# A hybrid transformer layer on one core: the residual gates multiply results in place of the weights w_out and w_down

## The chip, the cores and the metric

The kernel runs on one core of a Trainium2 chip. The metric is the time of one execution on the device, in microseconds (us); the median of several executions is compared.

The core's engines run side by side, each through a fixed list of instructions of its own: TensorE (PE in the profile; PEld is its weight load) does matmuls into PSUM, VectorE (DVE), ScalarE (ACT) and GpSimd (POOL) work element by element, and SyncE (SP) issues the DMA transfers, in the order of its list: a transfer whose turn has come but whose buffer is not free holds up all that stand behind it.

## The reference, cut to what matters

One layer on 2048 latent positions of 1024 channels, in float32:

```python
ada = jnp.einsum('bd,lde->lbe', jax.nn.silu(c), w_ada) + b_ada[:, None, :]
sh1, sc1, g1, sh2, sc2, g2 = (m[:, None, :] for m in jnp.split(ada[l], 6, axis=-1))
...
h = modulate(rmsnorm(x, norm_mix[l]), sh1, sc1)
o, _, _ = token_mixers(h @ w_in[l], ...)              # gated recurrence, and a spatial gating unit
x = x + g1 * (o @ w_out[l])                           # w_out: 1024 x 1024
h2 = modulate(rmsnorm(x, norm_ffn[l]), sh2, sc2)
x = x + g2 * conv_ffn(h2, w_up[l], conv_w[l], conv_b[l], w_down[l], rows)   # w_down: 2816 x 1024
...
return rmsnorm(x, norm_final)
```

g1 and g2 are vectors over the 1024 output channels. So g1 * (o @ w_out) is the same as o @ (w_out * g1), each column of the weight being multiplied by its gate, and likewise for g2 and w_down.

## The kernel before, in words

Each float32 product is made of three matmuls on split operands: `split(hi, lo, raw)` lets ACT round a tile to `hi` (a CAST) and another engine, POOL unless one is named, subtract: `lo = raw - hi`; `mm3` then adds up hi x hi, hi x lo and lo x hi. A right operand is 512 columns wide.

The work is done in stages.

- Stage 1 (0 to about 1036 us): input projection, the recurrence's heads and the gating unit's heads. The weights of w_in are split in 128x1024 tiles (`whi`, `wlo`); the results, transposed, go to DRAM (`oT`). Behind it runs a background queue, `bg_q`, a list of generators that are advanced as the matmuls are written out: a number that a generator yields is the amount of PE time to let pass before its next step. It holds `ada_block` (the gates; g1 and g2 end up in DRAM as the two rows of `g_d`), `w_out_ops`, `conv_taps` and `w_down_ops`.
- `w_out_ops` loads w_out in sixteen 128x512 pieces, each with a broadcast of its part of g1, multiplies (DVE), splits (ACT, DVE) and stores both halves to DRAM (`wo_d`). `w_down_ops` loads w_down in 22 pieces of 128x1024, multiplies by g2 (DVE) and stores them to `wd_d`.
- The handover: `open_wo` opens the pool for the output projection. The split w_out, eight tiles `wo` of 1 MB (128 rows of w_out each, both halves), is loaded from `wo_d`, three of them early, into buffers that the heads have left (`wo_early`). The first tile of `o` is loaded through a raw buffer and split by ACT and DVE.
- The output projection (1036 to 1230): 16 tiles of 128 positions; in each, two halves of the columns (n) and in each half eight k, with three matmuls each: 48 matmuls `dn<-wo,o`. DVE adds the result to x (`xn`, shown as `cv<-dn,raw`), SP stores it, ACT squares it (L1255). After every second tile `second_norm` follows: POOL makes `rs`, DVE scales both tiles of `xn` (L1176), PE transposes them (`up<-ident,cv`, or `dn<-ident,cv` for the last pair), and the results, split, are stored as `yd`, from where the far operands `yl` and `yh` are loaded.
- The up-projection and the convolution (1230 to 2108) are not touched.
- The down-projection (2108 to 2533): by a scheme with seven products of half sums, in seven phases (q = 0 to 6) of NJ = 11 steps with 8 result tiles each. `load` fetches the operands of a step three steps ahead, `prepare` forms the sums and differences of two weight blocks (`sT`, in a ring `wr()` of five, or a resident one) and activations (`mr`, `sS`) and splits them (`mhl`, `th`, `tl`). After the last step of a phase `evict` adds the 8 results to `odd` or `even` rows, `sums_behind` and `odd_rows` do the rest in the steps that follow.

The order of the instructions on each engine is fixed when the program is built, by a scheduler that follows the order in which they are written and a model of the time that passes.

Of the kernel before, what the change touches and what calls it, by code (L numbers as in the profile page):

```python
# [18 lines left out]
P = 128  # L19
# [53 lines left out]
def tile_trunk(ctx, tc, x, c, cx, c_ctx, w_ada, b_ada, norm_mix, norm_ffn, w_in, hg_norm, sgu_g, sgu_b,  # L73
# [31 lines left out]
    xl_d = dr.tile([P, NK, TH], F32, name="xl_d")  # L105
    wo_d = dr.tile([P, NK, 2, D], F32, name="wo_d")
    wd_d = [dr.tile([P, 2, D], F32, name=f"wd{j}") for j in range(NF // 2)]
    xn_d = [dr.tile([P, D], F32, name=f"xn{i}") for i in range(2 * NCH)]
# [69 lines left out]
    with es1:  # L178
# [634 lines left out]

        def wo_load(t):
            ld(t.bitcast(F32), wo_d[:, len(wo)])
            wo.append(t)

        def wo_early(tag):
            wo_load(pk.tile([P, 2, D], F32R, tag=tag, name="wo", bufs=2 if tag == "K" else 1, align_bytes=AL))

# [67 lines left out]

        def w_out_ops():

            todo = [(k, slice(n * 512, n * 512 + 512)) for k in range(NK) for n in range(2)]
            raws = []

            def load(i):
                if i < len(todo):
                    k, cl = todo[i]
                    raw = raw_tile()
                    ld(raw[:, :512], w_out[k * P:(k + 1) * P, cl])
                    ld(raw[:, 512:], g_d[0:1, cl].broadcast_to([P, 512]))
                    raws.append(raw)  # L900
            load(0)
            yield 5.0
            for i, (k, cl) in enumerate(todo):
                load(i + 1)
                raw = raws.pop(0)
                w, g = raw[:, :512], raw[:, 512:]
                hi = pm.tile([P, 512], F32, tag="acc", name="wo_hi")
                pin(V.tensor_mul(w, w, g))
                split(hi.bitcast(F32R), g.bitcast(F32R), w, V)
                st(wo_d[:, k, 0, cl], hi)  # L910
                st(wo_d[:, k, 1, cl], g)
                yield 7.0

        def w_down_ops():

            for n in range(2):
                cl = slice(n * 512, n * 512 + 512)
                g = pm.tile([P, 512], F32, tag="acc", name="g2")
                ld(g, g_d[1:2, cl].broadcast_to([P, 512]))
                for j in range(NF // 2):  # L920
                    raw = raw_tile().rearrange("p (a c) -> p a c", a=2)
                    ld(raw, w_down[2 * j * P:2 * (j + 1) * P, cl].rearrange("(a p) c -> p a c", p=P))
                    yield 9.0
                    pin(V.tensor_mul(raw, raw, view(g, 0, [[0, 2], [1, 512]])))
                    st(wd_d[j][:, :, cl], raw)
                    yield 2.5

        def silu(dst, scale):
# [6 lines left out]
        def head(hh, h):  # L935
# [16 lines left out]
            def pre_g():  # L952
                if prev[0] >= 0:
                    need(hg_q, (prev[0], prev[1], "keys"))
                else:
                    need(bg_q, "x1")
                    for e in range(8):
                        bg_q.add(ada_block(e))
                    bg_q.add(w_out_ops())
                    bg_q.add(conv_taps())  # L960
                    bg_q.add(w_down_ops())
                t["F"] = pk.tile([P, 2, TH], F32, tag="F", name="F", align_bytes=AL)
                t["K"] = pk.tile([P, 2, TH], F32, tag="K", name="K", bufs=2, align_bytes=AL)
# [77 lines left out]
        def open_wo():  # L1041
            hg_q.drain()
            bg_q.drain()
            esh.close()
            pw = esw.enter_context(tc.tile_pool(name="pw", bufs=1, side="right", reuse_waits="tile"))
            first_o.append(lambda: pw.tile([P, 2, NK, P], F32R, tag="o", name="o", align_bytes=AL))
            early = len(wo)

            def load():
                raw = raw_tile().rearrange("p (k c) -> p k c", c=P)  # L1050
                ld(raw, oT_d[0][:, :, 0:P])
# [119 lines left out]
    with tc.tile_pool(name="po", bufs=1, reuse_waits="tile") as po:  # L1171
# [49 lines left out]
        def fetch_x(t):  # L1221
            xt = raw_tile2(2 if t == nt_ - 1 else 1 + 2 * (t % 2))
            ld(xt.rearrange("p a b -> p (a b)"), x[t * P:(t + 1) * P, :])
            return xt.rearrange("p a b -> p (a b)")

        raw_o = {1: fetch_o(1)}
        xts = {0: fetch_x(0)}
        ops = {0: first_o[1]}
        xs = []
        for t, (hh, g) in enumerate(tiles):  # L1230
# [21 lines left out]
            xn = v_tile()[:, :D]  # L1252
            V.tensor_add(xn, pd.rearrange("p a b -> p (a b)"), xts.pop(t))
            st(xn_d[t], xn)
# [167 lines left out]
    def b_src(c, n, j):  # L1422
        return wd_d[j][:, c, n * 512:(n + 1) * 512]

# [82 lines left out]
    even = [pd_.tile([P, 2, 512], F32, name=f"even{i}") for i in range(NCH)]  # L1507
    nf = pd_.tile([P, D], F32, name="nf")
    nw = [0]
    ra, rb = {}, {}  # L1510
# [52 lines left out]
    def prepare(n):  # L1563

        if n >= 7 * NJ:
            return
        q, j = divmod(n, NJ)
        (a, b), (a2_, b2) = ra.pop(n), rb.pop(n, (None, None))
        if q == 4:
            V.tensor_sub(a, a, a2_)  # L1570
            V.tensor_sub(b, b, b2)
        cast(n, a, b, slot_s(n), slot_t(n))
        S_, T_ = sS[:, j, :], sTj(j)
        if q == 1:
            V.tensor_add(S_, a2_, S_)
            V.tensor_sub(T_, b2, T_)
        elif q == 2:
            V.tensor_sub(S_, S_, a2_)
            V.tensor_sub(T_, b2, T_)
        elif q == 3:  # L1580
            V.tensor_sub(S_, a2_, S_)
        elif q == 5:
            V.tensor_sub(T_, T_, b2)
# [45 lines left out]
    def sums_behind(q, i):  # L1629
        o, e = odd[i], even[i]  # L1630
        if q == 1:
            side.append(lambda: V.tensor_add(e[:, 0, :], e[:, 0, :], o[:, 0, :]))
        elif q == 3:
            def f():
                V.tensor_add(e[:, 1, :], e[:, 1, :], o[:, 0, :])
                V.tensor_add(e[:, 1, :], e[:, 1, :], o[:, 1, :])
            side.append(f)
        elif q == 4:
            def f():
# [14 lines left out]
    def evict(q, i, pd):  # L1654
        o, e = odd[i], even[i]
        if q in (0, 2):
            S.copy(o[:, q // 2, :], pd)
        elif q in (1, 5):
            V.tensor_add(e[:, q // 5, :], pd, e[:, q // 5, :])
        elif q in (3, 4):  # L1660
            V.tensor_add(o[:, 0, :], pd, o[:, 0, :])
# [65 lines left out]
```

## Time and profile before

| | us |
|---|---|
| median of 3 executions | 2530.53 |
| lowest, highest | 2528.71, 2533.55 |
| span of the profiled execution | 2532.6 |
| PE busy | 2450.9 (97%) |
| DVE busy | 1802.1 (71%) |
| POOL busy | 1063.7 (42%) |
| ACT busy | 960.3 (38%) |

The DMA queues move 400.13 MB. A time of the profiled execution by itself is not listed; its span, from the first to the last instruction, lies 0.95 below the highest of the three times and 2.1 above their median. Busy time is read as a share of the span: with PE at 97%, what is left for a change that keeps the matmuls is PE's idle time and the stretches in which the clock that PE was granted is below full.

### The profile page before, as it was taken

What the parts mean: (1) busy time and instruction counts of PE and PEld (TensorE: products, weight loads), DVE (VectorE), ACT (ScalarE), POOL (GpSimd) and SP (SyncE); (2) the same over time, 40 slices, a digit from 0 to 9 for tenths busy, and PEclk for the clock granted to TensorE, in tenths of its full rate; (3) what the DMA queues carried; (4) which work ended last, traced back from release to release, by engine and by line L of the source; (5) the groups of instructions that cost most, each with busy time, mean ns of one, the idle gap of its engine ahead of it and who ended that gap; (6) DMA issues with size and microseconds to landing.
All of it is one profiled execution on the core that took longest, in us unless ns stands there. A gap on an engine that the chain in (4) does not pass through costs nothing.

```text
span 2532.6 us, 32806 instructions
## 1 busy us (share of the span) xinstructions
PE 2450.9 (97%) x11859; PEld 2022.7 (80%) x11859; DVE 1802.1 (71%) x2375; ACT 960.3 (38%) x1598; POOL 1063.7 (42%) x871
## 2 busy tenths in 40 slices
PE   7999999999999999999999999999999999999998
PEld 4788888878888888788778888878878887888786
DVE  5866775735756757465699778749999993676775
ACT  2554334434334333255443333324333342332252
POOL 1444232322333433100587887877878870000002
PEclk8999999999999999999999999999999999999999
DMA  8365334583353422667932222472222248844744
GB/s 291 100 190 175 118 116 157 182 293 112 112 163 112 153 96 88 225 220 248 309 101 89 89 84 89 140 267 84 81 91 92 88 144 331 275 144 139 227 155 149
DMA packets 305838, 400.13 MB, mean 158 GB/s; under 512 B 33025, under 2 KB 216057, under 8 KB 301965
## 3 DMA queue, kind: packets, MB, share of 16 engines
q1 hardware_dynamic: 302420, 397.30, 47.4%
q8 instruction: 94, 1.54, 0.2%
q10 hardware_dynamic: 3257, 0.75, 0.1%
q14 instruction: 67, 0.55, 0.1%
HBM read 288.85 MB, written 109.13 MB: 157 GB/s over the span
## 4 chain that ended last, share of the span: by engine, by line
PE 39%; DVE 6%; DMA 2%; POOL 2%; issue 1%; ACT 0%; SPq 0%; POOLq 0%; ACTq 0%; DVEq 0%
PE up L65 24%; PE dn L65 15%; DVE dn L1315 3%; DVE edges L1320 1%; DMA raw<-in_w_up_dram 1%; DMA sT<-wd 1%; POOL Al L121 1%; DVE gp L1391 0%; DMA yl<-yd 0%; POOL cv L1402 0%; DVE odd L1595 0%; DMA mr<-m 0%; POOL raw L1142 0%; ACT dn L1612 0%; DVE cv L1399 0%
## 5 line engine op out<-in xcount | busy, mean ns | idle before, releaser
L1315 DVE SCALAR_TENSOR_TENSOR dn<-gp,taps,dn 128x1024 f32<-128x1024 f32 x352 | 448.2, 1280 | 20.5 <-ACT dn L1312 17.3
L121 POOL TENSOR_TENSOR Al<-raw,Ah 128x512 fp32r<-128x512 f32 x264 | 344.8, 1313 | 97.4 <-ACT Ah L120 88.9
L65 PE MATMUL pj<-xh,whi 128*128 128x512 f32 x896 | 366.4, 409 | 2.1 <-ACT whi L120 1.6
L65 PE MATMUL pj<-xl,whi 128*128 128x512 f32 x896 | 353.4, 395 | 3.7 <-DMA xl<-xl_d 1.8
L65 PE MATMUL pj<-xh,wlo 128*128 128x512 f32 x896 | 353.2, 394 | 2.7 <-POOL wlo L121 1.7
L65 PE MATMUL dn<-th,mhl 128*128 128x512 f32 x1120 | 349.9, 393 | 4.4 <-ACT mhl L120 2.4
L65 PE MATMUL up<-xah,Ah 128*128 128x512 f32 x704 | 277.5, 394 | 1.7 <-ACT Ah L120 1.3
L65 PE MATMUL up<-xah,Al 128*128 128x512 f32 x704 | 276.8, 393 | 2.0 <-POOL Al L121 2.0
L65 PE MATMUL up<-yl,Ah 128*128 128x512 f32 x704 | 274.6, 390 | 2.1 <-DMA yl<-yd 2.1
L120 ACT CAST Ah<-raw 128x512 fp32r<-128x512 f32 x264 | 160.4, 618 | 295.9 <-PE up L65 243.5
L65 PEld LDWEIGHTS dn<-th,mhl 128*128 128x128 f32 x1120 | 211.7, 189 | 50.7 <-ACT mhl L120 2.8
L121 POOL TENSOR_TENSOR wlo<-raw,whi 128x1024 fp32r<-128x1024 f32 x56 | 144.1, 2574 | 243.2 <-ACT whi L120 198.2
L113 POOL TENSOR_SCALAR rs<-ss 128x2 f32<-128x2 f32 (+1 forms) x16 | 7.7, 479 | 534.4 <-ACT jk L1587 366.0
L65 PE MATMUL dn<-tl,mhl 128*128 128x512 f32 x560 | 220.6, 394 | 0.0
L65 PE MATMUL up<-yh,Ah 128*128 128x512 f32 x528 | 208.1, 394 | 0.0
L65 PE MATMUL up<-yh,Al 128*128 128x512 f32 x528 | 206.9, 392 | 0.0
L65 PE MATMUL up<-xal,Ah 128*128 128x512 f32 x528 | 206.2, 391 | 0.0
L65 PEld LDWEIGHTS pj<-xh,wlo 128*128 128x128 f32 x896 | 169.4, 189 | 39.5 <-POOL wlo L121 2.2
L65 PEld LDWEIGHTS pj<-xh,whi 128*128 128x128 f32 x896 | 169.8, 189 | 36.8 <-issue 3.8
L65 PEld LDWEIGHTS pj<-xl,whi 128*128 128x128 f32 x896 | 169.8, 190 | 36.4 <-DMA xl<-xl_d 3.2
L65 PE MATMUL dn<-wo,o 128*128 128x512 f32 x768 | 184.6, 396 | 2.4 <-DMA wo<-wo_d 1.5
L65 PEld LDWEIGHTS dn<-wo,o 128*128 128x128 f32 x768 | 142.8, 189 | 32.7 <-DMA wo<-wo_d 2.0
(321 smaller groups left out, 4674.1 us busy)
## 6 DMA issues: line engine op xcount, KB each, us to landing
raw<-in_w_up_dram SPq DMA_DIRECT2D x88, 512.0 KB
mr<-m SPq DMA_DIRECT2D x85, 512.0 KB
raw<-in_w_in_dram SPq DMA_DIRECT2D x68, 512.0 KB
sT<-wd SPq DMA_DIRECT2D x88, 256.0 KB
raw<-in_w_ada_dram SPq DMA_DIRECT2D x32, 512.0 KB
m<-cv SPq DMA_DIRECT2D x22, 544.0 KB
raw<-in_w_down_dram SPq DMA_DIRECT2D x22, 512.0 KB
wd<-raw SPq DMA_DIRECT2D x22, 512.0 KB
```

What stands on the lines that cost most here:

```text
L65: return self.engine.matmul(out, lhsT, rhs, **kw)
L113: keep(G.tensor_scalar(out=r[:, :n], in0=ss, scalar1=scale, scalar2=bias, op0=ALU.mult, op1=ALU.add))
L120: keep(S.copy(hi, raw))
L121: (eng or G).tensor_sub(lo, raw, hi.bitcast(F32))
L1315: V.scalar_tensor_tensor(out=cr, in0=gt[:, t // 3:t // 3 + RH, t % 3:t % 3 + GW], scalar=taps[:, t * NF + f:t * NF + f + 1], in1=cr, op0=A ...
L1320: V.scalar_tensor_tensor(out=e[:, 0, :], in0=gt[:, 1, t % 3:t % 3 + GW], scalar=taps[:, t * NF + f:t * NF + f + 1], in1=e[:, 0, :], op0=AL ...
```

## The change

The gates g1 and g2 no longer multiply the weights. `w_out_ops` and `w_down_ops`, `wo_d` and `wd_d` are gone. `open_wo` loads w_out itself in eight 512 KB pieces through the ring of three raw buffers (one of which holds the first `o`), and splits them by ACT and POOL, one step of the background queue each. In the output projection DVE multiplies each half of the result by g1 and then adds x. The down-projection reads w_down; in phases 5 and 6 `prepare` multiplies the raw weight block by g2, since their results are added to rows that are already multiplied, and for the results of the earlier phases `even_rows` and `odd_rows` multiply sums by g2 (one half of the odd rows on POOL). The rows of `xn` for the even results are loaded by halves after phases 1 and 3, and no longer by whole tiles early in phase 0.

```diff
-        def wo_load(t):
-            ld(t.bitcast(F32), wo_d[:, len(wo)])
-            wo.append(t)
...
-        def w_out_ops():
...
-                pin(V.tensor_mul(w, w, g))
-                split(hi.bitcast(F32R), g.bitcast(F32R), w, V)
-                st(wo_d[:, k, 0, cl], hi)
-                st(wo_d[:, k, 1, cl], g)
-                yield 7.0
-
-        def w_down_ops():
...
-                    pin(V.tensor_mul(raw, raw, view(g, 0, [[0, 2], [1, 512]])))
-                    st(wd_d[j][:, :, cl], raw)
-                    yield 2.5
...
+            def fetch(k):
+                if k < NK:
+                    raws.append(raw_tile())
+                    ld(raws[-1], w_out[k * P:(k + 1) * P, :])
 
             def load():
...
-                for k in range(early, NK):
-                    wo_load(pw.tile([P, 2, D], F32R, name=f"wo{k}", align_bytes=AL))
-                yield 17.0
-                o = first_o[0]()
-                split(o[:, 0], o[:, 1], raw, V, pin)
-                first_o.append(o)
-                yield 0.0
+                fetch(0)
+                fetch(1)
+                yield 4.0
+                for k in range(NK):
+                    if k == 3:
+                        o = first_o[0]()
+                        split(o[:, 0], o[:, 1], ro, V, pin)
+                        first_o.append(o)
+                    split(wo[k][:, 0, :], wo[k][:, 1, :], raws.pop(0))
+                    fetch(k + 2)
+                    yield 2.2
...
+        g1 = [t[:, :4, :].bitcast(F32).rearrange("p a b -> p (a b)") for t in a_tiles()]
+        for n in range(2):
+            ld(g1[n], g_d[0:1, n * 512:n * 512 + 512].broadcast_to([P, 512]))
...
-            V.tensor_add(xn, pd.rearrange("p a b -> p (a b)"), xts.pop(t))
+            for n in range(2):
+                V.tensor_mul(xn[:, n * 512:n * 512 + 512], pd[:, n, :], g1[n])
+            V.tensor_add(xn, xn, xts.pop(t))
...
-        return wd_d[j][:, c, n * 512:(n + 1) * 512]
+        return w_down[(2 * j + c) * P:(2 * j + c + 1) * P, n * 512:(n + 1) * 512]
...
+        if q > 4:
+            cl = slice(512 * (6 - q), 512 * (6 - q) + 512)
+            V.tensor_mul(b, b, g2[:, cl])
         cast(n, a, b, slot_s(n), slot_t(n))
...
+    def even_rows(i, n):
+        e = even[i][:, n, :]
+        if n:
+            V.tensor_add(e, odd[i][:, 0, :], odd[i][:, 1, :])
+        V.tensor_mul(e, e, g2[:, n * 512:n * 512 + 512])
+        V.tensor_add(e, e, xts.pop(i))
...
+        for n, eng in enumerate((V, G)):
+            eng.tensor_mul(o[:, n, :], o[:, n, :], g2[:, n * 512:n * 512 + 512])
         V.tensor_add(flat(o), flat(o), xts.pop(i))
...
-        elif q in (1, 5):
-            V.tensor_add(e[:, q // 5, :], pd, e[:, q // 5, :])
+        elif q == 1:
+            V.tensor_add(e[:, 0, :], pd, o[:, 0, :])
+        elif q == 5:
+            V.tensor_add(e[:, 1, :], pd, e[:, 1, :])
...
-        if n in range(4, 4 + NCH):
-            ld(flat(even[n - 4]), xn_d[n - 4])
+        if n == NJ:
+            ld(g2, g_d[1:2, :].broadcast_to([P, D]))
```

Three places in the order of the built programs follow (line numbers of the changed kernel are two lower in the helpers, so that L119 there is L121 before).

POOL at the handover, before: `nt` is the last gate products of stage 1, `rs` and `mhalf` belong to norms, and behind the last `nt` the norms of the output projection follow at once.

```order
L641 TENSOR_TENSOR nt<-nt,gu 128x512
L113 TENSOR_SCALAR rs<-mv 128x4
L115 TENSOR_TENSOR rs_8350<-rs,mhalf 128x4
L641 TENSOR_TENSOR nt<-nt,gu 128x512
L113 TENSOR_SCALAR rs<-ss 128x2
```

The same place in the change; `wo<-raw,wo` is the subtraction that makes the low half of a piece of w_out:

```order
L639 TENSOR_TENSOR nt<-nt,gu 128x512
L111 TENSOR_SCALAR rs<-mv 128x4
L113 TENSOR_TENSOR rs_8117<-rs,mhalf 128x4
L119 TENSOR_TENSOR wo<-raw,wo 128x1024 x2
L639 TENSOR_TENSOR nt<-nt,gu 128x512
L119 TENSOR_TENSOR wo<-raw,wo 128x1024
L119 TENSOR_TENSOR wo_7976<-raw,wo_7976 128x1024
L119 TENSOR_TENSOR wo_7977<-raw,wo_7977 128x1024
L119 TENSOR_TENSOR wo_7978<-raw,wo_7978 128x1024
L119 TENSOR_TENSOR wo_7979<-raw,wo_7979 128x1024
L119 TENSOR_TENSOR wo_7980<-raw,wo_7980 128x1024
L111 TENSOR_SCALAR rs<-ss 128x2
```

Eight subtractions now stand on POOL around stage 1's last `nt`; before there were none.

PE in the third tile of the output projection (second half), before: the transposes of the pair that has just ended (`up<-ident,cv`) stand between the matmuls of the tile.

```order
L65 MATMUL dn<-wo,o 128x512 x3
L69 MATMUL up<-ident,cv 128x128 x4
L65 MATMUL dn<-wo,o 128x512 x6
L65 MATMUL dn<-wo_8227,o 128x512 x3
L65 MATMUL dn<-wo_8229,o 128x512 x3
```

And in the change:

```order
L65 MATMUL dn<-wo,o 128x512 x3
L69 MATMUL up<-ident,cv 128x128
L65 MATMUL dn<-wo,o 128x512 x3
L69 MATMUL up<-ident,cv 128x128 x3
L65 MATMUL dn<-wo,o 128x512 x3
L65 MATMUL dn<-wo_7976,o 128x512 x3
```

Three of the first four transposes are moved behind three more matmuls; the first has stayed.

DVE at the end of phase 4 of the down-projection, before: the loads of the weight blocks `sT` are used by L1583 (the next difference), and L1661 is the eviction of phase 4's results.

```order
L1583 TENSOR_TENSOR sT<-sT 128x512 x2
L121 TENSOR_TENSOR mhl<-sS,mhl 128x1024
L121 TENSOR_TENSOR tl<-sT,th 128x512
L1583 TENSOR_TENSOR sT<-sT 128x512
L121 TENSOR_TENSOR mhl<-sS,mhl 128x1024
L121 TENSOR_TENSOR tl<-sT,th 128x512
L1661 TENSOR_TENSOR odd_17206<-dn,odd_17206 128x512
L1661 TENSOR_TENSOR odd_17207<-dn,odd_17207 128x512
```

In the change (L1544 is the product with g2, whose tile is called `g_17035` here, L1556 the difference and L1647 the eviction):

```order
L1544 TENSOR_TENSOR sT<-sT,g_17035 128x512
L1556 TENSOR_TENSOR sT<-sT 128x512 x2
L1544 TENSOR_TENSOR sT<-sT,g_17035 128x512 x2
L119 TENSOR_TENSOR mhl<-sS,mhl 128x1024
L119 TENSOR_TENSOR tl<-sT,th 128x512
L1544 TENSOR_TENSOR sT<-sT,g_17035 128x512 x4
L1647 TENSOR_TENSOR odd_17018<-dn,odd_17018 128x512
L119 TENSOR_TENSOR mhl<-sS,mhl 128x1024
L119 TENSOR_TENSOR tl<-sT,th 128x512
L1647 TENSOR_TENSOR odd_17019<-dn,odd_17019 128x512
```

Products with g2 have come in ahead of the first eviction, and one pair of subtractions between the first two evictions.

More of the change, by code (lines that the diff above doesn't have):

```diff
@@ L105, in tile_trunk @@
     xl_d = dr.tile([P, NK, TH], F32, name="xl_d")
-    wo_d = dr.tile([P, NK, 2, D], F32, name="wo_d")
-    wd_d = [dr.tile([P, 2, D], F32, name=f"wd{j}") for j in range(NF // 2)]
     xn_d = [dr.tile([P, D], F32, name=f"xn{i}") for i in range(2 * NCH)]
@@ L812, in tile_trunk @@
         wo = []
-        def wo_load(t):
-            ld(t.bitcast(F32), wo_d[:, len(wo)])
-            wo.append(t)
         def wo_early(tag):
-            wo_load(pk.tile([P, 2, D], F32R, tag=tag, name="wo", bufs=2 if tag == "K" else 1, align_bytes=AL))
+            wo.append(pk.tile([P, 2, D], F32R, tag=tag, name="wo", bufs=2 if tag == "K" else 1, align_bytes=AL))
         def deferred(h):
@@ L887, in ada_block @@
             yield 0.0
-        def w_out_ops():
[L891 to L908, printed above, removed]
-                split(hi.bitcast(F32R), g.bitcast(F32R), w, V)
-                st(wo_d[:, k, 0, cl], hi)
-                st(wo_d[:, k, 1, cl], g)
-                yield 7.0
-        def w_down_ops():
[L916 to L924, printed above, removed]
-                    st(wd_d[j][:, :, cl], raw)
-                    yield 2.5
         def silu(dst, scale):
@@ L1046, in open_wo @@
             first_o.append(lambda: pw.tile([P, 2, NK, P], F32R, tag="o", name="o", align_bytes=AL))
-            early = len(wo)
-            def load():
-                raw = raw_tile().rearrange("p (k c) -> p k c", c=P)
-                ld(raw, oT_d[0][:, :, 0:P])
-                for k in range(early, NK):
-                    wo_load(pw.tile([P, 2, D], F32R, name=f"wo{k}", align_bytes=AL))
-                yield 17.0
-                o = first_o[0]()
-                split(o[:, 0], o[:, 1], raw, V, pin)
-                first_o.append(o)
-                yield 0.0
+            raws = []
+            def fetch(k):
+                if k < NK:
+                    raws.append(raw_tile())
+                    ld(raws[-1], w_out[k * P:(k + 1) * P, :])
+            def load():
+                ro = raw_tile().rearrange("p (k c) -> p k c", c=P)
+                ld(ro, oT_d[0][:, :, 0:P])
+                for k in range(len(wo), NK):
+                    wo.append(pw.tile([P, 2, D], F32R, name=f"wo{k}", align_bytes=AL))
+                fetch(0)
[9 more added lines that the diff above has]
+                    yield 2.2
             bg_q.add(load())
@@ L1508, in tile_trunk @@
     nf = pd_.tile([P, D], F32, name="nf")
+    g2 = pd_.tile([P, D], F32, name="g2")
     nw = [0]
```

14 lines of the change are left out of this document (7 added, 7 removed).

## The prediction

> **What bounds the kernel now.** I read the page's first table, then busy time and granted clock by stretches (windows), then the timeline wherever a stretch of PE was not full, then the cost of the instructions that go.
>
> ```profile
> span 2532.6 us, 32806 instructions
> ...
> PE 2450.9 (97%) x11859; PEld 2022.7 (80%) x11859; DVE 1802.1 (71%) x2375; ACT 960.3 (38%) x1598; POOL 1063.7 (42%) x871
> ```
>
> PE is the bound: 97% of 2532.6 us. The change leaves PE's matmuls as they are, so all it can move is the 82 us in which PE idles and the time in which its clock is halved. Columns below: stretch, length, busy us of PE, PEld, DVE, ACT, POOL (instructions), granted clock, DMA share, GB/s.
>
> ```profile
> 400.00:500.00 100.00, 97.45 (x543) 83.69 (x542) 63.83 (x96) 42.16 (x63) 29.65 (x18) 1.00 0.52 171
> 500.00:600.00 100.00, 91.81 (x471) 75.83 (x469) 52.75 (x67) 37.11 (x54) 28.77 (x15) 0.97 0.65 220
> 600.00:700.00 100.00, 98.17 (x568) 85.72 (x569) 63.50 (x82) 39.86 (x61) 27.29 (x15) 1.00 0.38 126
> 700.00:800.00 100.00, 98.08 (x556) 84.82 (x555) 67.85 (x91) 38.45 (x81) 39.91 (x25) 1.00 0.44 146
> 800.00:900.00 100.00, 96.70 (x564) 83.81 (x564) 65.51 (x94) 41.59 (x88) 30.35 (x20) 1.00 0.40 131
> ...
> 1036.40:1039.80 3.40, 3.27 (x7) 2.31 (x8) 1.16 (x2) 0.00 (x0) 2.13 (x1) 0.50 1.02 431
> ...
> 2150.00:2390.00 240.00, 240.00 (x1050) 196.93 (x1049) 171.30 (x203) 76.65 (x103) 0.00 (x0) 1.00 0.63 205
> 2390.00:2420.00 30.00, 28.01 (x116) 22.53 (x115) 25.62 (x35) 10.44 (x18) 0.00 (x0) 0.94 0.52 151
> ```
>
> Four places matter: stage 1 from 400 to 900, where the gate work on w_out and w_down runs behind the matmuls; the handover to the output projection at 1036; that projection and its end; and the down-projection.
>
> **Stage 1: what goes.** These are the removed groups (min/median/max ns of one).
>
> ```profile
> L908 DVE TENSOR_TENSOR raw<-raw x16: 670/682/696, 426.1 to 556.8; 128x512 f32<-128x512 f32 x16
> L121 DVE TENSOR_TENSOR raw<-raw,wo_hi x16: 691/692/2036, 427.5 to 558.2; 128x512 fp32r<-128x512 f32 x16
> L924 DVE TENSOR_TENSOR raw<-raw,g x22: 1205/1216/3418, 583.8 to 891.4; 128x1024 f32<-128x1024 f32 x22
> ```
>
> By the medians that is 16 x 0.68 + 16 x 0.69 + 22 x 1.22 = 49 us of DVE, and at DVE's 53 to 68% busy in those windows it is no bound by itself. It is worth what it makes PE wait. PE's waits in the worst hundred us:
>
> ```profile
> 539.99 0.50 PE L65 MATMUL pj<-xl,whi 128*128 128x512 f32 x1 [0.55 <-DMA xl<-xl_d]
> ...
> 556.78 0.50 PE L65 MATMUL pj<-xh,whi 128*128 128x512 f32 x1 [1.62 <-ACT whi L120]
> 559.72 0.79 PE L65 MATMUL pj<-xh,wlo 128*128 128x512 f32 x1 [1.72 <-POOL wlo L121]
> 570.60 2.19 PE L65 MATMUL sc<-Q,K 128*128 128x128 f32 x16 [1.37 <-ACT K L548]
> ```
>
> Late loads (xl_d, and the weight behind whi and wlo) are what a queue full of w_out transfers gives, so 0.55 + 1.62 + 1.72 = 3.9 us may go, and with them the clock's loss, 0.03 x 100 = 3 us. Two bounds: nothing goes, since the heads' own chains (ACT K) are late too; or the whole idle above the level of 600 to 700 goes, (2.55 + 8.19 + 1.83 + 1.92 + 3.30) - 5 x 1.83 = 8.6 us, and the 3 us of clock, 12 in all. I take 6, nearest to the rows that name a load. Stores and reloads of wo_d and wd_d go too; their reloads later are replaced by reads of the raw weights, of half the size for w_out and the same for w_down, and at a DMA share of 0.63 in the down-projection they bound nothing.
>
> **The handover: the first cost.** Before, wo arrives already split. Now eight splits (an ACT cast and a POOL subtraction of 128x1024 each) stand on the spot. The order of POOL puts two of them behind the last rs, then the gate product nt, then six.
>
> ```profile
> L121 POOL TENSOR_TENSOR wlo<-raw,whi x56: 2361/2403/5566, 36.0 to 980.0; 128x1024 fp32r<-128x1024 f32 x56
> L121 POOL TENSOR_TENSOR wlo<-raw,whi 128x1024 fp32r<-128x1024 f32 x56 | 144.1, 2574 | 243.2 <-ACT whi L120 198.2
> ```
>
> And the timeline at the handover (start us, us, engine, line; in brackets the idle time before it and what ended it):
>
> ```profile
> 1031.04 1.28 POOL L641 TENSOR_TENSOR nt<-nt,gu 128x512 f32<-128x512 f32 x1 [3.11 <-DVE mv L661]
> ...
> 1032.68 1.01 POOL L115 TENSOR_TENSOR rs<-rs,mhalf 128x4 f32<-128x4 f32 x1
> 1034.19 1.45 PE L65 MATMUL mi<-wsT,nt 128*128 128x128 f32 x8 [1.10 <-DVE nt L665]
> ...
> 1036.34 1.22 DVE L121 TENSOR_TENSOR o<-raw,o 128x1024 fp32r<-128x1024 f32 x1
> 1036.53 6.69 PE L65 MATMUL dn<-wo,o 128*128 128x512 f32 x21 [0.89 <-issue]
> 1044.75 1.43 PE L65 MATMUL dn<-wo,o 128*128 128x512 f32 x5 [1.53 <-DMA wo<-wo_d]
> ...
> 1050.11 0.53 SPq L1213 DMA_DIRECT2D raw<-oT  x1
> ...
> 1053.57 1.03 ACT L120 CAST o<-raw 128x1024 fp32r<-128x1024 f32 x1
> ...
> 1225.67 4.49 PE L65 MATMUL dn<-wo,o 128*128 128x512 f32 x19
> ```
>
> POOL is free from 1032.68 + 1.01 = 1033.7. Two subtractions of 2.40 end at 1038.5, nt (1.28) at 1039.8. The third needs its raw tile, whose slot is freed by DVE's subtraction of o: some 1036.3, then 3.4 us of load (1050.11 to 1053.57 for the same 512 KB) and a cast of 1.03, so 1040.8. Six times 2.40 from there: the last piece of wo is there at 1055.2. From then on the three slots of the raw ring leave each load 4.8 us against the 4.5 it needs, so POOL sets the pace. PE needs that piece as the eighth of its first half tile (21 matmuls come before it), and had it at 1044.75. So PE stands still 10.4 us longer, in bits of about 1.7 us after every three matmuls: 3 x 0.24 us at full clock (4.49 / 19 by the last row) against 2.40.
>
> Then the clock. The window 1036.4 to 1039.8 shows that it is granted at 0.50 behind idle stretches of no more than 0.9 and 1.1 us; the paced stretch has longer ones. Such a window costs 1.7 us, and the 27 matmuls left of tile 0 (27 x 0.24 = 6.4 us) can hold one or two: +1.7 or +3.4. I take +1.7, so +12 for the handover. Its lower end is 8 subtractions at the minimum, 0.04 x 8 earlier, the third not waiting (0.9) and no clock: +9; its upper end takes 2.57 us for one (the group's mean, in its second row) and two windows: 10.4 + 8 x 0.17 + 3.4 = +15.
>
> The Trainium skill, "TensorE: Matmul & The Clock Gate", section "What's actually happening", says that the clock is halved after at least one idle window of about 3.4 us. By that rule a PE that gets three matmuls every 2.4 us might never be throttled, and the handover would be 10.4; by the rows it is 12. The row of 1036.4 decides for me, since no idle stretch ahead of it comes near 3.4 us.
>
> What follows is hidden: ACT's eight casts and the load of the second tile's o (queued behind the last split's slot: 1055 + 3.4 + 1.03 + 1.22 = 1060.7) end while PE works on the first tile until about 1063.
>
> **The output projection: the evictions.** Each tile's one addition on DVE becomes two products with g1 out of PSUM and an addition.
>
> ```profile
> 1157.70 1.23 DVE L1253 TENSOR_TENSOR cv<-dn,raw 128x1024 f32<-128x1024 f32 x1 [0.62 <-PE dn L65]
> ...
> 1163.07 0.75 DVE L1176 TENSOR_SCALAR cv<-cv,rs 128x1024 f32<-128x1024 f32 x1
> 1163.62 0.80 PE L69 MATMUL up<-ident,cv 128*128 128x128 f32 x4
> L1391 DVE TENSOR_TENSOR gp<-up,keep x88: 674/684/695, 1238.0 to 2047.0; 128x512 f32<-128x512 f32 x88
> ```
>
> The nearest product out of PSUM takes 0.68 us (L1391), so a tile's result is 2 x 0.68 = 1.4 us later; as DVE work, 16 x 1.4 = 22 us spread over 190, it runs beside PE's matmuls. As latency it is covered within a pair's first tile, but not at its second: square, rs and scale follow at once, and PE's second group of transposes starts as the scale ends (1163.07 + 0.75 = 1163.8, in the middle of the row 1163.62 that lasts to 1164.4). PE's order has moved them by three matmuls (0.7 us) in five of seven pairs, six or eight in the others. That leaves 1.4 - 0.7 = 0.7 us in five pairs: +3. Bounds: 0, if the slack is larger than this pair's, and 7 x 0.7 = +5.
>
> The last pair has no such shift: all four first transposes stand where one stood.
>
> ```profile
> 1230.46 0.51 SPq L1279 DMA_DIRECT2D yl<-yd  x1
> ...
> 1232.27 1.22 DVE L1253 TENSOR_TENSOR cv<-dn,raw 128x1024 f32<-128x1024 f32 x1
> 1233.41 1.09 DVE L121 TENSOR_TENSOR fl<-fl,yst 128x896 fp32r<-128x896 f32 x1
> 1234.94 0.67 SPq L1254 DMA_DIRECT2D xn<-cv  x1
> ...
> 1240.53 0.75 DVE L1176 TENSOR_SCALAR cv<-cv,rs 128x1024 f32<-128x1024 f32 x1 [1.04 <-DMA xn<-cv]
> 1241.34 0.55 PE L69 MATMUL dn<-ident,cv 128*128 128x128 f32 x3 [0.85 <-DVE cv L1176]
> ```
>
> DVE's order now puts the fl subtraction of 1233.41 ahead of the two products and a MEMSET ahead of the addition, so that this ends at 1234.5 + 2 x 0.68 + 1.22 = 1237.1 instead of 1233.5. The store of xn goes 2 us later, the last scale waits for it, and on SP the far loads of yl and yh, one of which was issued at 1230.46, ahead of this store, are all behind it. PE already waited 0.85 there; I take +3, between +1 (the delay of the addition less what SP and PE's order give) and +5 (3.6 us, and late loads).
>
> **The down-projection.** DVE gets 22 products of weights, and three more operations for each of eight even and odd rows: 46 x 0.68 = 31 us. At 171 of 240 us busy it has room. Where PE waits for DVE is one boundary:
>
> ```profile
> 2394.72 0.69 DVE L1583 TENSOR_TENSOR sT<-sT 128x512 f32<-128x512 f32 x1 [2.97 <-DMA sT<-wd]
> ...
> 2397.90 0.47 PE L65 MATMUL dn<-th,mhl 128*128 128x512 f32 x1 [1.99 <-DVE odd L1661]
> ```
>
> DVE sits in its order behind a late load of a weight, so the evictions of phase 4 come late. In the new order four products, each behind such a load, stand ahead of the first eviction, and a subtraction pair (mhl, tl) behind it. If the loads come early, as the removed xn loads let them, the wait and its clock loss (0.06 of 30 us) go: -2.0 - 1.8 = -3.8. If not, 4 x 0.68 + 1.22 + 0.68 come on top: +4.6. Between these I take 0: the same load still ends the wait.
>
> **The sum.** -6 + 12 + 3 + 3 + 0 = +12 us. The rows are of an execution with a span of 2532.6, 0.9 below the highest of the three times (2533.55) and 2.1 above their median, 2530.5; the sum is a difference and is carried over to the median: 2542.5, slower by 0.47%. Less than 0.2% (5 us) is what a measurement of this kernel can't tell from no change.
>
> **The rivals.**
> *Faster by the freed background.* The matmul counts in the windows speak for it: 568 in 600 to 700, but 543, 471, 556 and 564 in the others; if all of that is due to gate work, 25 + 97 + 12 + 4 = 138 matmuls, at 568 in 100 us, are 24 us. Then -24 + 18 = -6: 2524. It decides once stage 1 gives over 23. Against it: the mix of shapes changes with the heads, and ACT K and DVE nt, heads' own work, end waits in the same stretch. Chance 0.13.
> *No change.* Stage 1 gives its 12, and the handover costs its lower end of 9 with the clock up: -12 + 9 + 3 + 3 = +3, 2533. For it: splits of 2.36 us exist. Against: the halved row at 1036.4. Chance 0.22.
> *Slower by much more.* The q4 to q5 boundary gets its upper bound and the last pair's far loads, at a DMA that is full, delay the weights behind them: +12 + 4.6 + 5 = +22, 2552. DVE's late sT loads speak for it; the removed xn loads against. Chance 0.15.
> *The forecast,* +6 to +18: 0.50.
>
> **How the numbers follow.** Likeliest 2542.5, its own range 2536 to 2549. The 8-in-10 range runs from 2528, between the faster rival and no change, to 2555, the sum of the upper ends with a stage 1 that gives little. Faster 0.13, within 0.2% 0.22, slower 0.50 + 0.15 = 0.65.
>
> **What would show it.** Right: PE idle between about 1036 and 1055 in bits of 1.7 us, released by POOL wo; that clock near 0.5; 540 to 565 without late loads; short waits for DVE cv in the projection's pairs. Wrong: the last wo there by 1047; stage 1 ending over 12 us earlier than 1036; or a new wait in the down-projection, where 46 products turn out not to be covered.

## The result, and the profile after

| | before | changed |
|---|---|---|
| median, us | 2532.04 (4 executions) | 2549.14 (4 executions) |
| lowest to highest, us | 2528.71 to 2536.44 | 2546.13 to 2554.86 |
| span of the profiled execution, us | 2532.6 | 2553.1 |

The ratio is 1.0071, with a 95% interval of 1.0053 to 1.0089: the change costs 17 us (by the interval 13 to 23), where +12 was forecast. The profiled execution of the changed kernel is its slowest (2554.9; mean clock 0.983, that of the others 0.986 to 0.987), so the two profiles differ by 20.5 us where the medians differ by 17.1.

The head of the page after:

```profile
span 2553.1 us, 32672 instructions
...
PE 2463.8 (97%) x11859; PEld 2029.9 (80%) x11859; DVE 1800.8 (71%) x2399; ACT 960.8 (38%) x1590; POOL 1101.2 (43%) x887
```

PE's matmuls are the same 11859. To see where time was lost, I set the start of the same matmul in both traces side by side; the last column is how far the difference moved since the row above. Each column is one execution: some steps differ by up to 3 us between traces of kernels that agree in what they do there, so a small one says little without the traces of the experiments.

| matmul | before, us | after, us | difference | moved by |
|---|---|---|---|---|
| first of the output projection | 1036.53 | 1029.13 | -7.40 | -7.4 stage 1 |
| first of its second tile | 1051.00 | 1054.19 | +3.20 | +10.6 handover |
| its last | 1229.77 | 1237.67 | +7.90 | +4.7 evictions |
| 309th of the up-projection | 1308.43 | 1320.04 | +11.61 | +3.7 last pair |
| last of the up-projection | 2089.03 | 2102.60 | +13.57 | +2.0 |
| first of phase 5 of the down-projection | 2397.90 | 2408.43 | +10.54 | -3.0 |
| last of the program | 2520.40 | 2540.74 | +20.34 | +9.8 phases 5 and 6 |

The windows after (columns as before):

```profile
400.00:500.00 100.00, 97.45 (x529) 83.31 (x529) 52.89 (x79) 37.49 (x54) 28.17 (x17) 0.98 0.25 80
500.00:600.00 100.00, 98.59 (x557) 85.17 (x556) 47.45 (x63) 39.01 (x58) 31.59 (x16) 1.00 0.41 140
...
1026.40:1050.40 24.00, 16.88 (x36) 10.45 (x37) 1.58 (x4) 6.28 (x6) 17.79 (x8) 0.50 0.59 196
2390.00:2420.00 30.00, 29.60 (x130) 23.97 (x129) 27.49 (x41) 8.05 (x10) 3.71 (x1) 1.00 0.60 206
2440.00:2460.00 20.00, 17.77 (x71) 14.07 (x70) 20.00 (x23) 6.24 (x12) 7.21 (x3) 0.92 0.41 145
2460.00:2480.00 20.00, 16.51 (x68) 12.95 (x67) 19.92 (x30) 10.38 (x18) 1.21 (x3) 0.93 0.35 116
```

The hundred us from 500 are full now: 557 matmuls where there were 471. The 24 us of the handover ran at half clock from end to end, with 36 matmuls. And from 2440 to 2480 DVE is busy for 39.9 of 40 us and PE for 34.3. Before, PE was full there and DVE was not:

```profile
2440.00:2460.00 20.00, 20.00 (x90) 16.38 (x88) 12.59 (x17) 8.99 (x14) 1.19 (x3) 1.00 0.19 61
2460.00:2480.00 20.00, 20.00 (x89) 16.42 (x88) 17.35 (x19) 13.41 (x21) 11.49 (x14) 1.00 0.65 234
```

The places of PE's waits after, us in total, times, longest:

```profile
PE dn L65 <- POOL wo L119: 5.6, 6, 1.3
PE up L69 <- DVE cv L1140: 5.0, 7, 1.4
...
PE up L65 <- DMA yl<-yd: 3.3, 2, 2.7
PE dn L69 <- DVE cv L1140: 2.6, 2, 1.7
...
PE dn L65 <- DVE tl L119: 2.2, 1, 2.2
PE dn L65 <- ACT th L118: 2.2, 1, 2.2
```

The first is the handover, the second the pairs of the output projection, the fourth the last pair; the last two are new, in phases 5 and 6. The handover in the timeline after:

```profile
1023.16 5.63 POOL L119 TENSOR_TENSOR wo<-raw,wo 128x1024 fp32r<-128x1024 f32 x2
1023.87 2.72 DVE L119 TENSOR_TENSOR o<-raw,o 128x1024 fp32r<-128x1024 f32 x1
...
1026.97 1.22 PE L65 MATMUL mi<-wsT,nt 128*128 128x128 f32 x4 [2.47 <-DVE nt L663]
1029.13 3.32 PE L65 MATMUL dn<-wo,o 128*128 128x512 f32 x7 [0.94 <-DVE nt L671]
...
1036.03 1.65 PE L65 MATMUL dn<-wo,o 128*128 128x512 f32 x3 [0.69 <-POOL wo L119]
1038.36 1.65 PE L65 MATMUL dn<-wo,o 128*128 128x512 f32 x3 [0.68 <-POOL wo L119]
...
1041.44 4.81 POOL L119 TENSOR_TENSOR wo<-raw,wo 128x1024 fp32r<-128x1024 f32 x2 [0.56 <-ACT wo L118]
```

PE gets three matmuls per 2.33 us (1036.03 to 1038.36), as POOL delivers. The first two rows show something else: DVE's subtraction of o, 1.22 us before, took 2.72 beside two subtractions on POOL. Before, it came behind the last `nt` on DVE; now some of these stand behind it, PE waits 2.47 us for them, and the clock falls to 0.50.

### The profile page after: what moved, and what is told of

Same layout as the page of the kernel before. It is cut to its first block, busy times and chain, and to the rows that moved or that the text cites. A ratio compares the mean times of both kernels' runs of the same rounds, so it can differ in the third digit from the quotient of the medians.

```text
span 2553.1 us, 32672 instructions
## 1 busy us (share of the span) xinstructions
PE 2463.8 (97%) x11859; PEld 2029.9 (80%) x11859; DVE 1800.8 (71%) x2399; ACT 960.8 (38%) x1590; POOL 1101.2 (43%) x887
## 5 line engine op out<-in xcount | busy, mean ns | idle before, releaser
L1284 DVE SCALAR_TENSOR_TENSOR dn<-gp,taps,dn 128x1024 f32<-128x1024 f32 x352 | 448.2, 1280 | 20.5 <-ACT dn L1281 17.3
L119 POOL TENSOR_TENSOR Al<-raw,Ah 128x512 fp32r<-128x512 f32 x264 | 344.1, 1310 | 113.9 <-ACT Ah L118 103.5
L119 POOL TENSOR_TENSOR wlo<-raw,whi 128x1024 fp32r<-128x1024 f32 x56 | 143.0, 2554 | 239.5 <-ACT whi L118 207.8
L65 PE MATMUL dn<-wo,o 128*128 128x512 f32 x768 | 192.2, 406 | 6.6 <-POOL wo L119 5.6
L1584 POOL TENSOR_TENSOR odd<-odd,g 128x512 f32<-128x512 f32 x8 | 20.4, 2565 | 327.0 <-DVE odd L1624 327.0
```

Of the source, the lines that this page charges most:

```text
L65: return self.engine.matmul(out, lhsT, rhs, **kw)
L119: (eng or G).tensor_sub(lo, raw, hi.bitcast(F32))
L1284: V.scalar_tensor_tensor(out=cr, in0=gt[:, t // 3:t // 3 + RH, t % 3:t % 3 + GW], scalar=taps[:, t * NF + f:t * NF + f + 1], in1=cr, op0=A ...
L1584: eng.tensor_mul(o[:, n, :], o[:, n, :], g2[:, n * 512:n * 512 + 512])
```

## Experiments

Each is given as an edit, what was expected, and what was measured; ratios are against the kernel before, on the same chip, with a 95% interval. All lie within 2% of it; faster or slower means here that the interval leaves out 1. The chips differ from run to run (the medians of before lie between 2532.0 and 2534.1), so differences of 1 or 2 us between the times of two experiments mean nothing. An edit also lets the scheduler move instructions near it. "Theory A" is the prediction's list of places.

**The w_out half alone.** `w_down_ops`, `wd_d` and the down-projection are those of before.

> Only the w_out half of the change (w_down is still multiplied by g2 in stage 1 and read from wd_d). Theory A, the places add up one by one: stage 1 gives back 12 us, since only the w_out transfers met the reload of xh and xl at 525 to 556; the handover takes 10 to 11, the evictions of the output projection 5, the last pair 3 to 4: about +8 us against before, 2540, with the end of the down-projection as before. Rival B, the freed SP queue and DVE time of w_down made the room in stage 1: then the output projection does not start earlier than before here, and the kernel is slower than before by 18 or more.

Measured: 1.0038 (1.0026 to 1.005), 2542.8 us. Between two matmuls at about 416 and 945 us it is 9.2 us quicker than before (the changed kernel: 11.9); the handover costs 11.7, the evictions 5.2. Stage 1's gain belongs to w_out: theory A, rival B falls. The last pair costs 0.6 us here, not 3 to 4.

**The w_down half alone.**

> Only the w_down half of the change (w_out is still multiplied and split in stage 1). Theory A: stage 1, handover and output projection as before within 1 us; the products and the xn halves of phases 5 and 6 leave DVE no room, so the last 100 us take 6 to 10 us longer, less 2 to 4 at the boundary from phase 4 to 5: +4 to +8 us, about 2537. Rival B: stage 1 becomes 5 us or more shorter, and the sum is within 3 us of before or below it.

Measured: 1.0021 (1.001 to 1.0032), 2537.3 us. The output projection starts 0.5 us earlier than before, and at the end of the up-projection the difference is 0.1 us; at phase 5 it is 4.1 us ahead, at the end 3.7 us behind. That is theory A. The two halves' costs add up within the intervals, 0.0038 + 0.0021 against 0.0071, and phases 5 and 6 cost 7.8 us here too.

**Every second subtraction of the handover on DVE.**

```diff
-                    split(wo[k][:, 0, :], wo[k][:, 1, :], raws.pop(0))
+                    split(wo[k][:, 0, :], wo[k][:, 1, :], raws.pop(0), V if k % 2 else G)
```

> The changed kernel, with every second subtraction of the handover's eight splits on DVE (1.22 us a piece there) and not on POOL. Theory A, POOL's 2.4 us a piece set the pace in which PE got w_out: the pieces come every 1.3 to 2 us and the handover shrinks by 5 to 8 us, to about 2542. Rival C, the ring of three raw buffers (load 3.4, cast 1.04, subtraction) or ACT sets the pace: no more than 1 us is gained, 2548.

Measured: 1.0053 (1.004 to 1.0066), 2545.6 us. From its first matmul to the second tile the output projection lost 8.8 us against before, where the changed kernel lost 10.6: 1.8 back, less than theory A's 5 to 8 and more than rival C's 1. POOL's pace alone is not the bound. ACT's casts wait for their load, as most of them do in the changed kernel:

```profile
1032.42 1.05 ACT L118 CAST wo<-raw 128x1024 fp32r<-128x1024 f32 x1 [2.44 <-DMA raw<-in_w_out_dram]
...
1036.93 1.04 ACT L118 CAST wo<-raw 128x1024 fp32r<-128x1024 f32 x1 [1.71 <-DMA raw<-in_w_out_dram]
```

A load can be issued only when the subtraction that last read its buffer is done, so a slow piece on POOL delays the piece three further on, wherever that is subtracted.

**The kernel before, its w_out work paced faster.**

```diff
-                yield 7.0
+                yield 5.0
```

> The kernel before, with one number changed: after each of its 16 steps the background work on w_out yields 5.0 instead of 7.0 us, so that all its loads and stores stand on the DMA queue ahead of the reload of xh and xl. Theory A, stage 1 lost its 12 us where the two met (late xl, then a weight load 11 us in the queue, then the halved clock): 8 to 12 us faster than before, about 2521. Rival D, the loss came from the work itself (DVE products, ACT casts), wherever it stands: within 3 us of before, the wait only moves.

Measured: 0.9983 (0.9974 to 0.9992), 2527.2 us: some 4 us, between the two. The profiled execution took 2534.2 us, 7 over the median, so its trace doesn't show where the median's gain lies. In it the waits for xl and whi at 540 to 560 fell from 3.4 to 1.1 us (0.51 + 0.63), but the work now costs where it has gone: at the matmul that before started at 473.5 this kernel is 5.1 us behind, with a wait of 1.58 us for ACT K, one of 1.92 for DVE Q, and the halved clock after them. Between the matmuls at about 416 and 945 us it gains nothing on before. In this trace stage 1's loss moved with the work, as rival D has it.

**k outside, the halves inside, in the first tile of the changed kernel.**

```diff
-            for n in range(2):
-                for k in range(NK):
+            for n, k in [(n, k) for k in range(NK) for n in range(2)] if t == 0 else [(n, k) for n in range(2) for k in range(NK)]:
```

> The changed kernel; in the first tile of the output projection k runs outside and the two halves inside, so that each piece of w_out gives PE six matmuls (1.4 us) and not three as it arrives. Theory A, the handover costs what PE waits for pieces that come every 2.3 us: the last piece leaves 6 matmuls to do, not 27, so 21 x 0.24 = 5 us come back: about 2544 where the changed kernel had 2549, and the output projection's second tile starts 5 us earlier against its first matmul. Rival E, the loss is the halved clock, which stays for as long as the pieces are late: no more than 2 us come back.

Measured: 1.0054 (1.0039 to 1.007), 2547.2 us; 2.0 us less than the changed kernel, with intervals that overlap. The pieces do give six matmuls each, but the next thing is late:

```profile
1038.77 1.66 PE L65 MATMUL dn<-wo,o 128*128 128x512 f32 x6 [1.35 <-POOL wo L119]
1041.13 1.41 PE L65 MATMUL dn<-wo,o 128*128 128x512 f32 x5 [0.71 <-POOL wo L119]
1046.66 13.61 PE L65 MATMUL dn<-wo,o 128*128 128x512 f32 x50 [4.12 <-ACT o L118]
```

The load of the second tile's o stands behind the ring of raw buffers. In the changed kernel the rest of the first tile covers it; here PE waits 4.12 us for it. From its first matmul to the second tile it lost 8.3 us, where the changed kernel lost 10.6. So less than half of what theory A expected came back, and the rest went into a wait that the expectation didn't name. The time alone fits rival E, but its reason falls: from 1029.95 to 1043.60, while the pieces were late, the clock was at 1.00.

**The w_down half with the odd rows' product on DVE.**

```diff
-        for n, eng in enumerate((V, G)):
+        for n, eng in enumerate((V, V)):
             eng.tensor_mul(o[:, n, :], o[:, n, :], g2[:, n * 512:n * 512 + 512])
```

> The w_down half of the change alone (timed 2537.3 against 2532.7 for before), with both halves of the odd rows' product with g2 on DVE, none on POOL. Theory F, DVE has too much to do in phases 5 and 6: eight products of 0.68 us come to it, eight stretches of 1.1 us in which it is held up beside POOL go, so the end stays within 2 us of the w_down half alone. Rival G, it is the hold-up beside POOL (0.68 us lengthened to 1.78) that makes DVE late: the last 100 us get 4 us or more shorter, 2533 or below.

Measured: 0.997 (0.9958 to 0.9982), 2526.9 us: 10 us less than the half it was made from, and faster than before. That is rival G's time. The products in the w_down half (min/median/max ns):

```profile
L1599 POOL TENSOR_TENSOR odd<-odd,g x8: 1682/1750/9303, 2400.9 to 2442.0; 128x512 f32<-128x512 f32 x8
L1599 DVE TENSOR_TENSOR odd<-odd,g x8: 678/680/685, 2407.0 to 2446.5; 128x512 f32<-128x512 f32 x8
```

Windows 2400 to 2440 and 2440 to 2460 of the w_down half:

```profile
2400.00:2440.00 40.00, 40.00 (x176) 32.62 (x175) 39.57 (x46) 13.35 (x24) 26.73 (x7) 1.00 0.46 151
2440.00:2460.00 20.00, 14.80 (x64) 11.49 (x62) 19.04 (x26) 7.84 (x15) 3.72 (x2) 0.98 0.32 107
```

And with the products on DVE:

```profile
2400.00:2440.00 40.00, 40.00 (x177) 32.81 (x176) 40.00 (x55) 15.54 (x27) 0.00 (x0) 1.00 0.43 145
2440.00:2460.00 20.00, 20.00 (x89) 16.43 (x88) 19.54 (x27) 14.91 (x26) 4.51 (x6) 1.00 0.50 173
```

DVE is full in both. But beside POOL it gets through 46 instructions in 40 us, 6 of them products with g2 of the odd rows (4.08 us), and alone through 55, 16 of them such products (10.29 us): the other 39 or 40 are much the same work, and 6.2 us of products fit in on top. In the timeline of the w_down half single operations of 0.68 us last 1.78 while POOL is at it:

```profile
2405.31 1.78 DVE L1639 TENSOR_TENSOR odd<-odd 128x512 f32<-128x512 f32 x1
2407.01 0.68 DVE L1599 TENSOR_TENSOR odd<-odd,g 128x512 f32<-128x512 f32 x1
2407.17 1.68 POOL L1599 TENSOR_TENSOR odd<-odd,g 128x512 f32<-128x512 f32 x1 [0.63 <-DVE odd L1639]
2407.62 1.78 DVE L1559 TENSOR_TENSOR sT<-sT,g 128x512 f32<-128x512 f32 x1
```

Eight of DVE's operations in phases 5 and 6 are lengthened in this way, by some 7 us in all; with the products on DVE none is. One product on POOL lasts 9.3 us. From 2440 PE pays for it: 14.80 against 20.00 us busy. How much of that is DVE's lost time and how much the odd rows that come late from POOL was not separated: the edit takes away both.

**The same half with the 22 products of weight blocks left out.**

> The w_down half of the change alone, with the 22 products of weight blocks with g2 in phases 5 and 6 left out (that part of the result lacks its gate). Theory F, DVE's load: 22 x 0.68 = 15 us less on DVE in the 110 us in which it is full, so the waits of PE at 2440 to 2465 go, 6 to 8 us, and the gain at the boundary from phase 4 to 5 stays: 2529, below before. Rival H, late loads of the weights through the ring or the hold-up beside POOL: the waits stay, within 2 us of 2537.

Measured: 0.9984 (0.9973 to 0.9994), 2529.5 us. PE's waits at the end go as well, to 0.6 us in all, though POOL still has its products. So both hold: DVE has no slack in phase 5, and either 15 us of work less or the hold-up gone is enough. As an explanation of the loss, F alone falls, since the run before it took work to DVE and gained.

**The w_out half with results by halves.**

```diff
-            pd = dbank()
+            pd = [ubank(), ubank()]
...
+            xt = xts.pop(t)
             for n in range(2):
-                V.tensor_mul(xn[:, n * 512:n * 512 + 512], pd[:, n, :], g1[n])
-            V.tensor_add(xn, xn, xts.pop(t))
+                V.tensor_mul(xn[:, n * 512:n * 512 + 512], pd[n], g1[n])
+                V.tensor_add(xn[:, n * 512:n * 512 + 512], xn[:, n * 512:n * 512 + 512], xt[:, n * 512:n * 512 + 512])
```

The transposes take their PSUM tiles from `dbank` and ACT's squares go into `xt`.

> The w_out half of the change alone (timed 2542.8 against 2532.7 for before), with two 512-column PSUM tiles in place of one of 1024 for each result of the output projection, product and addition by halves, so that DVE works on the first half while PE fills the second; the scheduler also lets the two halves of the first tile take turns, by k. Theory A: the 0.6 us that PE waits in each pair for the scaled rows go, and the last pair's 1.5, so that the 5 us from the second tile to the end of the output projection come back; and the handover gives 4 to 5 us by the turns: 2533, level with before. Rival I: transposes now have two PSUM buffers and not four, and the waits in the pairs stay or grow: 2538 or above.

Measured: 1.005 (1.0037 to 1.0064), 2545.2 us, not to be told from the half it was made from (the intervals overlap), where theory A had 2533. No wait over 0.4 us is left in the first five pairs, which had 0.54 to 0.70 each: that part of theory A holds. What it gained was lost again in two places: 6.56 us of wait for the second tile's o (the same wait as with k outside), and the last pairs, where five waits for the scaled rows add up to 6.0 us (there were 1.70, 0.56, 1.48 and 0.93). Whether the two PSUM buffers make these was not tried by itself.

**The whole change with the odd rows on DVE, and with the handover on DVE as well.**

> The whole change, with one letter changed: both halves of the odd rows' product with g2 on DVE. Theory G, eight products on POOL and DVE's additions and subtractions hold each other up, and the waits of PE in phases 5 and 6 are what follows: as in the w_down half alone, about 10 us come back, 2549 to 2539, and the last 100 us have no wait of PE. Rival J, with the w_out half there too the end of the program is late for other reasons (its loads): under 4 us come back, 2545 or above.

> As the run before it in this call (whole change, odd rows on DVE), and all eight subtractions of the handover on DVE, none on POOL. Theory C, three raw buffers set the pace once the subtraction is short (load 3.4 + cast 1.04 + subtraction 1.22 = 5.7 us for three pieces, 1.9 each, where POOL gave one in 2.3 to 2.6): the handover takes 7 to 8 us where it took 10.6, about 2536. Theory A alone, POOL's subtraction was the pace: 1.22 us a piece, 8 us come back, 2531 or below.

The first: 1.0015 (1.0002 to 1.0027), 2537.8 us, 11 less than the change, with no wait of PE over 0.4 us after 2123: theory G. The second: 0.9995 (0.998 to 1.0009), 2531.9 us, level with before. Its handover lost 5.4 us where the first's lost 10.6, and the casts follow each other by (1034.31 - 1023.63) / 5 = 2.1 us, each behind its load:

```profile
1023.63 1.04 ACT L118 CAST wo<-raw 128x1024 fp32r<-128x1024 f32 x1 [4.31 <-DMA raw<-in_w_out_dram]
...
1034.31 1.04 ACT L118 CAST wo<-raw 128x1024 fp32r<-128x1024 f32 x1 [0.73 <-DMA raw<-in_w_out_dram]
```

That is near the ring's pace (1.9 expected). The handover's 5.4 lies between the two theories, 7 to 8 by C and 10.6 - 8 = 2.6 by A, and the time is nearer to A's 2531 than to C's 2536. So POOL's subtraction was about half of the cost, and the waits for loads make the ring the likely bound of what is left; a fourth raw buffer was not tried.

**The w_down half, odd rows on DVE, w_out work paced by 5.0.**

> The best so far, the w_down half with the odd rows on DVE (0.997 of before), and the w_out work of stage 1 paced by 5.0 in place of 7.0 us (0.9983 of before by itself). If both gains stand, 0.995 of before, about 2521; if the gain of the pace was chance of the clock windows, 0.997.

Measured: 0.9974 (0.9962 to 0.9986), 2526.2 us. The intervals of this and of 0.997 overlap: the gain of the pace does not show on top. The best version is the w_down half of the change with the odd rows' products on DVE, faster than before by 0.3%; the pace alone gave 0.2%.

## Why the prediction was right, and where its terms were off

The direction and the handover as its main cause were right, and the time lies in the range, 2528 to 2555, though just above the forecast's own, 2536 to 2549. That +12 came near 17 is in part luck: stage 1 gave more than was forecast, and the down-projection, counted at nothing, cost more. One of the signs of being wrong did come: a new wait in the down-projection. By terms, from the traces (their sum is +20.4):

- **Stage 1, -6; measured -7.4.** The agreement is luck. Between the matmuls at about 416 and 945 us the change gained 11.9 us, the working's upper bound and twice its choice. The waits of 540 to 560 are gone, as argued, and so is the halved clock behind them; the run that paced the w_out work faster says that the loss goes with that work. Then 5.3 us were lost again, of which 3.1 in a place that the working did not look at: DVE's subtraction of o now stands ahead of the last `nt` and is slowed by POOL's subtractions. The w_out half loses the same 3.1 there, and the version with every subtraction on DVE 2.8, so POOL's share in it is not shown. The other 2.2 were lost before that, where the clock is halved from 1012.8 for 3.4 us; the traces of the w_out half and of k outside have no such window.
- **The handover, +12; measured +10.6.** Waits of 0.7 to 1.3 us behind POOL's pieces are there. The predicted bits were 1.7 us; at half clock the three matmuls take 1.65 us and fill most of each 2.3. PE got the last piece some 8.6 us later after its first matmul than before (10.4 forecast), and the matmuls behind it took 2.0 longer (1.7 forecast). The clock stayed at 0.50 for 23.9 us, so the row of 1036.4 was the right one to go by, though the number alone, nearer to the 10.4 without a loss of clock, would not say so. The Trainium skill, "TensorE: Matmul & The Clock Gate", section "What's actually happening", has the clock go up after some 3.4 us of sustained work and down after an idle window of that length. The traces agree with the first, and not with an idle window in the strict sense. The clock changes in steps of 3.41 us here; it fell behind a step in which PE was still busy for 24% (1023.06 to 1026.47), stayed at 0.50 over six steps of 48 to 76%, and rose behind one of 100%. With k outside it stayed at 1.00 over steps of 60 to 83%, and fell behind one of 48%. That POOL alone set the pace did not hold: with POOL out of the way half of the 10.6 was left, behind the loads of the ring.
- **The pairs, +3; measured +4.7.** 0.6 us in five pairs, as worked out, and 1.4 in the pair after them: there, as for the last pair, DVE's order puts an fl subtraction ahead of the products. The rows of one pair were taken for all.

```profile
1188.69 1.09 DVE L119 TENSOR_TENSOR fl<-fl,yst 128x896 fp32r<-128x896 f32 x1 [1.05 <-ACT yst L118]
1189.70 0.68 DVE L1221 TENSOR_TENSOR cv<-dn,Ah 128x512 f32<-128x512 f32 x1
...
1195.49 0.30 PE L69 MATMUL up<-ident,cv 128*128 128x128 f32 x1 [1.44 <-DVE cv L1140]
```

- **The last pair, +3; measured +3.7.** This too is luck. Its two waits for the scaled rows are 2.6 us, where one of 0.85 was; the rest is mostly a clock halved for 6.8 us behind them. Other runs with the same two waits lost between 0.1 (every second subtraction on DVE) and 2.7 us (the whole change with odd rows on DVE) here.
- **The up-projection, nothing; measured +2.0.** A wait for yl of 2.7 us (2.1 before) and a longer window of halved clock behind it. The traces of the experiments have 1.8 to 2.9 us there, 2.9 in the one that only paces the kernel before, and the step lies between -0.3 and +3.0: the change is not shown to cost anything here.
- **The down-projection, 0 with bounds -3.8 and +4.6; measured -3.0 and +9.8, together +6.8.** The step that failed is "at 171 of 240 us busy it has room". The window 2150 to 2390 was the wrong cover: most of the new work lies in phases 5 and 6, and the row of 2390 to 2420, quoted for another purpose, had DVE at 25.62 of 30 us. And that one half of the odd rows goes to POOL has no price in the sum at all. It cost the most: eight products of 512 columns, about 10 us of the program (runs with the odd rows on DVE, alone and in the whole change). At the boundary from phase 4 to 5 the wait is gone, as the lower bound said, but it is gone in the w_out half as well, which leaves the down-projection as it was: that the new order removed it is not shown.

That POOL's products are the price is shown by the two runs that moved only those products; that they and DVE's operations hold each other up, by the lengthened rows. The Trainium skill, "SBUF — State Buffer", section "Who interferes with whom", states it as a rule: a DVE instruction with two SBUF inputs contends with a GpSimd instruction that reads SBUF. The traces agree: 0.68 us lengthened to 1.78 on DVE, 1.68 to 9.3 on POOL, and 1.22 to 2.72 at the handover. The rule was at hand for the prediction, where it would have been a reason not to leave eight products on POOL without a price.

## What to carry to other kernels

An idle engine is not a free one: before work is given to POOL, look at whether DVE is nearly full of operations on two SBUF tiles in the same stretch, and price both engines' instructions at the longest that the trace shows for such neighbours. Take the cover for new work from the windows in which it will run, not from the mean of the stage. When a tensor's preparation moves from the background to the point where it is used, its pace there is that of the slowest engine or, if that is longer, of load, cast and subtraction together divided by the number of buffers (2.4 against 2.3 us with POOL, by the rows here); and what stands behind it in the queue is late next.

## What the hardware showed that I had not expected

- A 512-column product on POOL took 1.68 to 9.3 us beside a full DVE (the w_down half; 1.30 to 6.38 in the changed kernel).
- PE's clock stayed at 0.50 for 23.9 us in a row (1026.47 to 1050.36), over seven waits of 0.7 to 1.3 us, and was back at 1.00 once the matmuls followed each other; with k outside the same sort of waits (0.6 to 1.35 us) found it at 1.00 and left it there until 1043.60.
- Where these windows fall differs between executions that do the same work there: the window of 1012.8 is in the trace of the changed kernel and, 3 us earlier, in that of the change with odd rows on DVE, and not in those of the w_out half and of k outside. A term of 2 or 3 us can't be read from one pair of traces.
